# A recorded decoder trunk: projections that may pass each other in the plan, an inverse by 8-blocks, and work moved from VectorE to ScalarE and GpSimd

## The chip, the cores and the metric

The kernel runs on one core of a Trainium2 chip. The metric is the device time of one execution in microseconds (us): three executions of the kernel before took 4351.48, 4353.93 and 4364.67 us, the median is 4353.93 us. The change is one set of edits to one file; the shapes, the inputs and the outputs stay the same.

## The reference

One layer of a decoder trunk with two branches that read the same normalised input: a gated delta net with 8 heads of 128 (below: G) and an RWKV-7 branch with 16 heads of 64 (below: R), for a prompt of 16 + 2048 tokens and for 8 sample sequences of 4 tokens. The parts that matter here:

```python
h = rmsnorm(x, ln1_w)
p = jnp.einsum('btd,de->bte', h, w_in)           # one projection, 10384 columns wide
# branch A: causal convolution of 4 taps and SiLU on q, k, v; q and k normalised; decay g, beta
lower = where(strict, einsum('bnhik,bnhjk->bnhij', k_beta, k) * decay, 0.0)
t_inv = triangular_solve(eye + lower, eye)       # the inverse of a 64x64 unit triangle per chunk and head
# per chunk of 64 tokens, one after the other, with a state per head:
v_new = u_c - w_c @ s;  o = q_c @ s + qk_c @ v_new;  s = s * exp(gl_c) + kt_c^T @ v_new
# branch B, per token:  S = S diag(exp w) - (S kk)(kk*a)^T + v k^T,  y = S r;  group norm, bonus, gate
merged = gA * (o_a @ w_out_a) + gB * (o_b @ w_out_b)
y = rmsnorm(x + merged @ w_out, lnf_w)
```

The kernel computes the matrix products of the projections with three products of rounded halves: a number x is split into a high part (the same number, rounded to the matmul's format) and a low part (x minus the high part).

## The kernel before

**Work.** The 2064 prompt tokens are padded to 33 chunks of 64 and cut into five segments of 6, 6, 7, 7 and 7 chunks; the first carries the sample tokens too. In each segment the hidden rows are transposed and split into high and low tiles (`hHL`). Then come units: four G units (two heads each) and eight R units (two heads each). A unit has a projection stage (stage P: 128-column tiles of `w_in`, 24 matmuls each, into a PSUM tile `ps_p`), a stage M (normalisation, the chunk matrices, the inverse) and a chain C that goes through the segment's chunks one after the other (`ps_g` for G, `ps_c` for R). Gates, the two output projections and the final one follow as projection tiles.

**Weights** (`w_half`, L983). In the first segment a half tile of weights comes as raw numbers (`wr`); ScalarE rounds it to `wh`, and the low part `wl` is `wr` minus `wh`, a 128x512 subtraction: on VectorE for the first half of each tile, on GpSimd for the second. Both parts are then written to DRAM, and later segments load them from there.

**The split** (`split`, L962) of a 128-row tile `sq`, `kb`, `y` or `ysq`: a rounding copy into `sh` and a subtraction into `sl`, both on VectorE; two matmuls with a matrix of ones sum them over the partitions.

**The inverse** (`send_blocks`, L1357, and `g_inv`, L1369). The diagonal 16x16 blocks of all chunks and both heads of a unit are sent through DRAM so that each lies in one partition: 48 or 56 partitions of 256 numbers (`iM`). The tile `iD` is loaded with the identity from the constants. VectorE negates `iM`, and then finds row i of the inverse from the rows above it:

```python
for i in range(1, 16):
    self.tt(tmp[:NB, 0:i, 0:i], a, b, ALU.mult)
    nc.vector.tensor_reduce(Dk[:NB, 0, i, 0:i], tmp[:NB, 0:i, 0:i], AX.X, ALU.add)
```

GpSimd writes the transposed blocks beside, both go back through DRAM into `Dn` and `Dt`, and four rounds of small matmuls (`ps_n`, `Z`) make the 64x64 inverse out of them.

**The decay tile** of a G unit (in `g_g2`, L1433) is `EP`: a row of cumulated decays is loaded from DRAM into all partitions (`EP<-gcd`), VectorE subtracts a column `GT`, GpSimd adds a mask, ScalarE takes the exponential, VectorE multiplies by beta (a second `EP<-EP,GT`).

**What sets the order.** The operations are not issued as they are written. They are recorded as nodes, and a planner (`Sched`) walks through a model of time: each node has a cost by its engine, a node is ready when its inputs are there in the model, and each engine takes its best ready node (`pick`, L825; for TensorE `pick_pe`, L833). Pools of buffers are part of it. The order that comes out is then issued (`replay`, L894), and on the chip each engine goes through its own list strictly in that order. All instructions therefore carry the line of `replay` in the profile (L903), and are told apart by the names of their tiles.

TensorE knows kinds of matmuls: kind F (projections and other full-array rounded ones) and the small kinds. When `pick_pe` has finished a run of small ones, or has none worth a turn, it takes the next node of a projection tile. Committed projection tiles stand in the queue `s.pq`, some three or four of them. Only the tile at the head is looked at, and of it only the first node not yet started:

```python
if s.pq:
    for x in s.pq[0].pe:
        if not x.started:
            if x.nd == 0 and (not x.allocs or s.can(x)):
                pn = x
            break
```

A projection tile has four nodes of six matmuls, two for each half of its weights. A low-rank tile of an R unit (`lora`, `loral`) has one node of two matmuls and needs no weight buffer of the pool.

Of the kernel before, what the change touches and what calls it, by code (L numbers as in the profile page):

```python
# [4 lines left out]
F32 = mybir.dt.float32  # L5
# [3 lines left out]
ALU = mybir.AluOpType  # L9
AX = mybir.AxisListType  # L10
# [17 lines left out]
SEGMAX = 7  # L28
NT = 30
# [98 lines left out]
def plan(seq):  # L128
# [5 lines left out]
    for i in range(nseg):  # L134
        n = base + (1 if i >= nseg - extra else 0)
        t0, t1 = c0 * 64, (c0 + n) * 64
        p = max(0, pad - t0)
        segs.append(dict(i=i, nch=n, T=n * 64, pad=p, nreal=n * 64 - p, r0=max(t0 - pad, 0), last=False, smp=(i == 0)))
        c0 += n
# [307 lines left out]
class Sched:  # L447
# [385 lines left out]
    def pick_pe(s):  # L833
# [57 lines left out]
TWAIT = 3.0  # L891

# [13 lines left out]
class Trunk:  # L906
# [76 lines left out]
    def w_half(self, key):  # L983
# [8 lines left out]
        else:  # L992
# [3 lines left out]
            self.tt(wl, raw, wh.bitcast(F32), ALU.subtract, self.nc.gpsimd if key[1] else self.nc.vector)  # L996
# [27 lines left out]
    def setup(self):  # L1024
# [11 lines left out]
    def g_setup(self):  # L1036
# [48 lines left out]
        self.wbd = [P.tile([128, 2, 128], F32, name=f"wbd{i}") for i in range(1)]  # L1085
        self.xo = [P.tile([128, 2, 64], F32, name=f"xo{i}") for i in range(2)]
# [282 lines left out]
    def g_inv(self, sg, u):  # L1369
# [5 lines left out]
        M = self.p_i.tile([128, 16, 16], F32, tag="iM", name="iM", bufs=1)  # L1375
        nc.sync.dma_start(M[:NB], ex)
        Dk = self.p_i.tile([128, 2, 16, 16], F32, tag="iD", name="iD", bufs=1)
        io = CONST_LAYOUT["ID16"][0]
# [3 lines left out]
        tmp = self.p_i.tile([128, 16, 16], F32, tag="iT", name="iT", bufs=1)  # L1382
# [958 lines left out]
```

## Time and profile before

| | |
|---|---|
| time, median of 3 runs | 4353.93 us (4351.48 to 4364.67) |
| the profiled execution: its own time, its span | 4371.86 us, 4370.1 us |
| TensorE, matmuls | 4066.9 us busy, 93% of the span |
| VectorE | 2726.3 us, 62% |
| ScalarE | 1965.2 us, 45% |
| GpSimd | 992.3 us, 23% |
| mean granted TensorE clock | 0.941 of full speed |

The profiled execution is one execution with its own time, which is 17.9 us above the median; the trace numbers below are all its own. The page gives the time that an engine was busy. A matmul that runs while the granted clock is at half counts as busy for twice as long, so TensorE's 93% holds both useful time and time lost to the clock. The names: PE is TensorE, PEld its weight load, DVE is VectorE, ACT is ScalarE, POOL is GpSimd, SP the engine that issues the transfers. The five segments end at about 1000, 1780, 2560, 3440 and 4370 us.

### The profile page before, as it was taken

The numbers are of one execution on the slowest core, as the hardware profiler recorded it, in microseconds if no ns is written. First come the engines' busy times: TensorE is split into PE (matmuls) and PEld (weight loads), VectorE is DVE, ScalarE is ACT, GpSimd is POOL, SyncE is SP. The second block draws the span as 40 slices with busy tenths as digits, with TensorE's granted clock in tenths as the row PEclk, the third lists the DMA queues.
The fourth block names the chain that finished last, engine by engine and source line by source line (L and its number), as shares of the span: only waits on it lengthen the run. The fifth ranks groups of instructions, "written<-read, shape, count | busy, mean of one in ns | idle before, by whom it ended". The sixth has DMA issues, their size and how long they took to land. (4 is left out here: it accounts for less than half of the span.)

```text
span 4370.1 us, 91290 instructions
## 1 busy us (share of the span) xinstructions
PE 4066.9 (93%) x32684; PEld 3485.0 (80%) x32684; DVE 2726.3 (62%) x7052; ACT 1965.2 (45%) x4842; POOL 992.3 (23%) x1972
## 2 busy tenths in 40 slices
PE   6888999888999999999999999998998999999998
PEld 6767777778888888888788889787887887778887
DVE  6888677756576754557666645676763456666622
ACT  6544444525444443445444433554443334554431
POOL 3434233413121121212212121121121112111210
PEclk9889788979999999999999999999999999999999
DMA  7636465758745456864445567544445775444467
GB/s 254 201 117 203 136 199 172 243 171 279 235 145 154 137 166 211 263 201 148 126 127 157 172 223 261 159 139 131 128 151 170 237 239 151 128 140 137 143 221 256
DMA packets 660688, 790.09 MB, mean 181 GB/s; under 512 B 251105, under 2 KB 347209, under 8 KB 660234
## 3 DMA queue, kind: packets, MB, share of 16 engines
q1 hardware_dynamic: 660234, 784.25, 57.5%
q8 instruction: 259, 4.24, 0.4%
q14 instruction: 195, 1.60, 0.1%
HBM read 602.29 MB, written 180.56 MB: 179 GB/s over the span
## 5 line engine op out<-in xcount | busy, mean ns | idle before, releaser
L903 PE MATMUL ps_p<-hHL,wh 128*128 128x448 f32 (+3 forms) x7760 | 1828.1, 373 | 30.7 <-ACT wh L903 10.3
L903 PEld LDWEIGHTS ps_p<-hHL,wh 128*128 128x128 f32 x7760 | 1421.3, 195 | 156.1 <-issue 28.3
L903 PE MATMUL ps_p<-hHL,wl 128*128 128x448 f32 (+3 forms) x3880 | 911.6, 358 | 4.9 <-DVE wl L903 2.9
L903 PEld LDWEIGHTS ps_p<-hHL,wl 128*128 128x128 f32 x3880 | 730.2, 193 | 39.0 <-DVE wl L903 3.7
L903 POOL COPY xo<-X 64x64 f32<-64x64 f32 x528 | 172.4, 327 | 809.6 <-ACT X L903 380.1
L903 DVE TENSOR_TENSOR iT<-iM,iD 56x1 f32<-56x1 f32 (+1 forms) x900 | 295.5, 328 | 75.0 <-DMA iD<-in_consts 58.5
L903 ACT COPY raw<-ps_p 128x448 f32<-128x448 f32 (+3 forms) x285 | 144.2, 506 | 343.2 <-PE ps_p L903 313.8
L903 DVE SCALAR_TENSOR_TENSOR cv<-raw,pv,cv 128x448 f32<-128x448 f32 (+1 forms) x360 | 259.3, 720 | 56.0 <-ACT cv L903 48.6
L903 DVE TENSOR_REDUCE iD<-iT 56x1 f32<-56x1 f32 (+1 forms) x900 | 205.1, 228 | 17.7
L903 POOL TENSOR_TENSOR wl<-wr,wh 128x512 fp32r<-128x512 f32 x105 | 149.0, 1419 | 212.0 <-ACT wh L903 137.5
L903 ACT ACTIVATE X<-ps_c 64x64 f32<-64x64 f32 x264 | 55.5, 216 | 289.0 <-PE ps_c L903 124.2
L903 ACT CAST wh<-wr 128x512 fp32r<-128x512 f32 x210 | 128.3, 613 | 77.6 <-DMA wr<-in_wt 21.8
L903 ACT ACTIVATE X<-ps_c,dc 64x64 f32<-64x64 f32 x224 | 68.7, 307 | 207.2 <-DVE X L903 106.4
L903 DVE TENSOR_SCALAR X<-ps_c,dc 64x64 f32<-64x64 f32 x224 | 64.9, 291 | 135.0 <-PE ps_c L903 98.0
L903 ACT ACTIVATE sig<-cv 128x448 f32<-128x448 f32 (+2 forms) x120 | 67.3, 561 | 177.7 <-DVE cv L903 175.9
L903 PE MATMUL ps_p<-mhl,wh 128*128 128x448 f32 (+2 forms) x640 | 141.5, 359 | 5.7 <-ACT wh L903 4.5
L903 DVE TENSOR_SCALAR X<-ps_c 64x64 f32<-64x64 f32 x264 | 58.8, 227 | 131.1 <-PE ps_c L903 88.9
L903 DVE TENSOR_TENSOR Z<-Dt,ps_n 128x336 f32<-128x336 f32 (+1 forms) x180 | 66.9, 372 | 115.5 <-PE ps_n L903 100.0
L903 PE MATMUL ps_g<-gs,cv 128*64 128x128 f32 x1056 | 122.2, 308 | 17.0 <-DVE wbd L903 8.4
L903 PEld LDWEIGHTS ps_n<-Z,Wp 64*64 64x64 f32 x3168 | 109.9, 143 | 24.8 <-issue 9.5
L903 PE MATMUL ps_a<-RH,LH 64*128 64x128 f32 x1056 | 129.3, 292 | 0.0
L903 PE MATMUL ps_n<-Z,Wp 64*64 64x16 f32 (+1 forms) x3168 | 120.3, 220 | 7.7 <-DVE Z L903 5.8
(337 smaller groups left out, 7444.1 us busy)
## 6 DMA issues: line engine op xcount, KB each, us to landing
wh<-wh SPq DMA_DIRECT2D x1050, 256.0 KB
wl<-wl SPq DMA_DIRECT2D x1050, 256.0 KB
wr<-in_wt SPq DMA_DIRECT2D x210, 256.0 KB
gl<-gt SPq DMA_DIRECT2D x72, 224.0 KB
gt<-gt SPq DMA_DIRECT2D x48, 224.0 KB
xt<-in_x_prompt SPq DMA_DIRECT2D x29, 256.0 KB
xt<-in_x_prompt SPq DMA_DIRECT2D x13, 512.0 KB
out_y_p<-xt SPq DMA_DIRECT2D x26, 256.0 KB
```

Source lines behind the costliest of these rows:

```text
L903: getattr(getattr(nc, eng), name)(*[g(x) for x in a], **{q: g(x) for q, x in k.items()})
```

## The change

- **Planner.** `pick_pe` goes through up to `LOOK = 9` tiles of the queue, which is all of it, and takes the first whose next node is ready. A ready tile may pass one that is not, also between the halves of a tile.
- **Weights of the first segment.** All 210 low parts are now GpSimd's, where 105 were VectorE's.
- **Split.** The rounding copy `sh` goes from VectorE to ScalarE.
- **Inverse.** Seven steps make the inverses of both 8x8 halves of a 16x16 block at once; two products of 8x8 blocks (each in two pieces of 256 numbers, each a multiplication and a reduction) make the part below the diagonal. That is 11 multiplications and 11 reductions in place of 15 and 15. The identity is no longer loaded: GpSimd clears `iD` and writes the ones. The negation of `iM`, which waits for the transfer, is GpSimd's too.
- **Decay tile.** The subtraction, which waits for the transfer `EP<-gcd`, goes to GpSimd, and the mask's addition to VectorE.
- The numbers of two buffers (`NXO`, `NWB`) and the segment with the sample tokens (`SMP`) get names, with the values as before.

```diff
@@ pick_pe
-            if s.pq:
-                for x in s.pq[0].pe:
-                    if not x.started:
-                        if x.nd == 0 and (not x.allocs or s.can(x)):
-                            pn = x
-                        break
+            for p in s.pq[:LOOK]:
+                x = next(x for x in p.pe if not x.started)
+                if x.nd == 0 and (not x.allocs or s.can(x)):
+                    pn = x
+                    break
+LOOK = 9
@@ split
-        self.nc.vector.tensor_copy(h[:, :n], x)
+        self.nc.scalar.copy(h[:, :n], x)
@@ w_half
-            self.tt(wl, raw, wh.bitcast(F32), ALU.subtract, self.nc.gpsimd if key[1] else self.nc.vector)
+            self.tt(wl, raw, wh.bitcast(F32), ALU.subtract, self.nc.gpsimd)
@@ g_inv
-        nc.sync.dma_start(Dk[:NB, 0].rearrange("p a b -> p (a b)"), self.I["consts"][:NB, io:io + 256])
+        nc.gpsimd.memset(D0, 0.0)
+        nc.gpsimd.memset(D0[:, 0:256:17], 1.0)
         yield
-        nc.vector.tensor_scalar(M[:NB], M[:NB], -1.0, None, ALU.mult)
+        self.tt(M, M, self.eps[:NB, 4:5].unsqueeze(2).to_broadcast([NB, 16, 16]), ALU.mult, nc.gpsimd)
-        for i in range(1, 16):
-            a = M[:NB, 0:i, i].unsqueeze(1).to_broadcast([NB, i, i])
-            b = Dk[:NB, 0, 0:i, 0:i].rearrange("p m c -> p c m")
-            self.tt(tmp[:NB, 0:i, 0:i], a, b, ALU.mult)
-            nc.vector.tensor_reduce(Dk[:NB, 0, i, 0:i], tmp[:NB, 0:i, 0:i], AX.X, ALU.add)
+        for i in range(1, 8):
+            for_a = M2[:, :, 0:i, i].unsqueeze(2).to_broadcast([NB, 2, i, i])
+            for_b = D2[:, :, 0:i, 0:i].rearrange("p h m c -> p h c m")
+            tv = tmp[:NB, 0:2, 0:i, 0:i]
+            self.tt(tv, for_a, for_b, ALU.mult)
+            nc.vector.tensor_reduce(D2[:, :, i, 0:i], tv, AX.X, ALU.add)
             if i % 4 == 3:
                 yield
+        for q in range(2):
+            tv = tmp[:NB]
+            self.tt(tv, M[:, 0:8, 8 + 4 * q:12 + 4 * q]...to_broadcast([NB, 4, 8, 8]),
+                    D[:, 0:8, 0:8]...to_broadcast([NB, 4, 8, 8]), ALU.mult)
+            nc.vector.tensor_reduce(Xt[:NB, 4 * q:4 * q + 4], tv, AX.X, ALU.add)
+        yield
+        for q in range(2):
+            tv = tmp[:NB]
+            self.tt(tv, D[:, 8 + 4 * q:12 + 4 * q, 8:16]...to_broadcast([NB, 4, 8, 8]),
+                    Xt[:NB]...to_broadcast([NB, 4, 8, 8]), ALU.mult)
+            nc.vector.tensor_reduce(D[:, 8 + 4 * q:12 + 4 * q, 0:8], tv, AX.X, ALU.add)
@@ g_g2
-                self.tt(E3, E3, GT[:, :n, p].unsqueeze(2).to_broadcast([128, n, 64]), ALU.subtract)
-                self.tt(E3, E3, self.cst("MNEG").unsqueeze(1).to_broadcast([128, n, 64]), ALU.add, nc.gpsimd)
+                self.tt(E3, E3, GT[:, :n, p].unsqueeze(2).to_broadcast([128, n, 64]), ALU.subtract, nc.gpsimd)
+                self.tt(E3, E3, self.cst("MNEG").unsqueeze(1).to_broadcast([128, n, 64]), ALU.add)
```

Since costs and engines change, the planner's order changes nearly everywhere. Three places show what the text below speaks of.

**VectorE, first segment, in the middle of an inverse.** Before, the steps of one inverse (`iT` the products, `iD` the sums) stand between the work of other units, with a weight's low part among them:

```order
L903 TENSOR_TENSOR iT<-iM,iD 48x5x5
L903 SCALAR_TENSOR_TENSOR cv<-raw,pv,cv 128x384
L903 TENSOR_SCALAR X<-ps_c,dc 64x64
L903 TENSOR_REDUCE iD<-iT 48x5
L903 TENSOR_TENSOR wl<-wr,wh 128x512
L903 TENSOR_TENSOR iT<-iM,iD 48x6x6
L903 COPY rR<-ps_c 128x64
L903 TENSOR_REDUCE iD<-iT 48x6
```

In the change the seventh step is the last of its kind and the block products follow (`iX` is the intermediate 8x8 block):

```order
L905 TENSOR_TENSOR iT<-iM,iD 48x2x7x7
L905 TENSOR_TENSOR LH<-kb,cs 64x6x64
L905 TENSOR_REDUCE iD<-iT 48x2x7
L905 TENSOR_TENSOR RH<-sq,E 128x6x64
L905 TENSOR_TENSOR iT<-iM,iD 48x256
L905 COPY wbd_259<-ps_g 64x128
L905 COPY rR<-ps_c 128x64
L905 TENSOR_REDUCE iX<-iT 48x32
```

No `wl` stands on VectorE any more, and no `sh`; the chain's own instructions (`rR`, `X`, `wbd`) still stand between the steps of an inverse, behind fewer of them.

**GpSimd, first segment, where the first R chain runs.** `xo` are copies of an R chain's state that TensorE reads, `carA`, `rs`, `cvo` belong to the convolution. Before:

```order
L903 TENSOR_TENSOR wl<-wr,wh 128x512
L903 COPY cvo<-rs 128x24
L903 MEMSET mx_z 128x48
L903 COPY xo_260<-X 64x64 x6
L903 COPY iD<-iD 48x256
L903 COPY rs<-cvi 128x8x3
```

And in the change:

```order
L905 TENSOR_TENSOR wl<-wr,wh 128x512
L905 COPY xo_260<-X 64x64 x2
L905 TENSOR_TENSOR wl<-wr,wh 128x512 x2
L905 MEMSET mx_z 128x48
L905 TENSOR_TENSOR wl<-wr,wh 128x512
L905 COPY iD<-iD 48x256
L905 TENSOR_TENSOR wl<-wr,wh 128x512
L905 COPY xo_260<-X 64x64 x2
```

Six `xo` copies that stood side by side now have one to four low parts between them, and the copies of an R chain wait behind these.

**TensorE, first segment, a low-rank tile.** Before (numbers of the buffers are shown), the tile `ps_p_4340` is done before `ps_p_4491` starts, and the next tile starts after that:

```order
L903 MATMUL ps_p_4340<-hHL_936,wl_4314 128x376
...
L903 MATMUL ps_g_4334<-wbd0_259,ktl_3526 128x256
L903 MATMUL ps_p_4491<-lora0_1259,w2_4079 128x416
L903 MATMUL ps_p_4491<-loral_1277,w2_4079 128x416
L903 MATMUL ps_a_4503<-sh_4396,onesR_254 128x416
L903 MATMUL ps_a_4503<-sl_4423,onesR_254 128x416
L903 MATMUL ps_p_4513<-hHL_922,wh_4353 128x376 x2
```

In the change the tile `ps_p_4710` is half done when the low-rank tile `ps_p_4768` passes it:

```order
L905 MATMUL ps_p_4710<-hHL_926,wl_4603 128x368
...
L905 MATMUL ps_a_4757<-rAMs_3313,rVs_2265 64x32 x2
L905 MATMUL ps_g_4633<-wbd0_259,ktl_3176 128x256
L905 MATMUL ps_p_4768<-lora1_1269,w2_4007 128x416
L905 MATMUL ps_p_4768<-loral_1322,w2_4007 128x416
L905 MATMUL ps_p_4710<-hHL_934,wh_4654 128x368 x2
L905 MATMUL ps_p_4710<-hHL_935,wh_4654 128x368 x2
```

In TensorE's whole order of the change 57 of 611 projection tiles are broken off and taken up again after another tile, and none is before; in 52 of the 57 it is one low-rank tile of two matmuls that passes.

## Rows read from the trace of the kernel before

**Rows 1.** page, part 1: engine, busy us (share of the span) xinstructions

```profile
PE 4066.9 (93%) x32684; PEld 3485.0 (80%) x32684; DVE 2726.3 (62%) x7052; ACT 1965.2 (45%) x4842; POOL 992.3 (23%) x1972
```

**Rows 2.** windows, whole core: stretch, length, busy us (xcount) by engine, clock, DMA, GB/s

```profile
0.00:110.00 110.00, 73.35 (x407) 67.50 (x407) 66.55 (x163) 66.45 (x165) 38.09 (x100) 0.97 0.78 255
...
110.00:440.00 330.00, 279.34 (x2153) 235.82 (x2153) 273.95 (x740) 160.43 (x379) 128.81 (x242) 0.86 0.55 173
...
440.00:1000.00 560.00, 514.31 (x4403) 427.43 (x4402) 366.64 (x971) 240.05 (x610) 166.38 (x282) 0.85 0.58 185
...
1000.00:4370.10 3370.10, 3199.92 (x25726) 2754.28 (x25725) 2019.17 (x5181) 1498.31 (x3691) 659.01 (x1348) 0.96 0.58 178
...
1000.00:1780.00 780.00, 722.37 (x5933) 636.10 (x5933) 478.04 (x1272) 359.08 (x920) 173.07 (x350) 0.95 0.61 189
```

**Rows 3.** waits of PE: tile, releaser and tile, us in total, times, longest

```profile
PE ps_c L903 <- DVE X L903: 26.9, 22, 4.3
...
PE ps_p L903 <- ACT wh L903: 14.7, 7, 7.2
...
PE ps_g L903 <- DVE gs L903: 0.3, 1, 0.3
```

**Rows 4.** groups of DVE: xcount | busy us, mean ns | idle before, releasers

```profile
L903 DVE TENSOR_TENSOR iT<-iM,iD 56x1 f32<-56x1 f32 (+1 forms) x900 | 295.5, 328 | 75.0 <-DMA iD<-in_consts 58.5
...
L903 DVE TENSOR_REDUCE iD<-iT 56x1 f32<-56x1 f32 (+1 forms) x900 | 205.1, 228 | 17.7
...
L903 DVE TENSOR_TENSOR wl<-wr,wh 128x512 fp32r<-128x512 f32 x105 | 80.8, 770 | 27.3 <-DMA wl<-wl 10.7 <-ACT wh L903 9.4 <-DMA wh<-wh 3.0
...
L903 DVE CAST sh<-sq 128x448 fp32r<-128x448 f32 (+2 forms) x120 | 53.4, 446 | 16.0 <-ACT sq L903 13.8 <-PE ps_a L903 1.6
...
L903 DVE TENSOR_SCALAR iM<-iM 56x256 f32<-56x256 f32 (+1 forms) x60 | 17.0, 283 | 70.2 <-DMA iM<-ex 69.8
...
L903 DVE CAST sh<-y 128x448 fp32r<-128x448 f32 (+2 forms) x40 | 16.2, 405 | 4.4 <-ACT y L903 3.6
```

**Rows 5.** groups of DVE with shapes kept apart: steps of the inverse

```profile
L903 DVE TENSOR_TENSOR iT<-iM,iD 56x225 f32<-56x225 f32 x36 | 19.9, 553 | 0.7
...
L903 DVE TENSOR_TENSOR iT<-iM,iD 56x100 f32<-56x100 f32 x36 | 11.9, 330 | 0.7
...
L903 DVE TENSOR_REDUCE iD<-iT 56x15 f32<-56x225 f32 x36 | 13.6, 377 | 0.9
```

**Rows 6.** groups of DVE, 0 to 1000 us, then 1000 to 1780 us

```profile
L903 DVE TENSOR_TENSOR iT<-iM,iD 48x1 f32<-48x1 f32 (+4 forms) x180 | 71.6, 398 | 11.9 <-DMA iD<-in_consts 9.9
...
L903 DVE TENSOR_TENSOR iT<-iM,iD 48x1 f32<-48x1 f32 (+4 forms) x180 | 55.2, 307 | 17.0 <-DMA iD<-in_consts 13.4
```

**Rows 7.** groups of POOL, whole span

```profile
L903 POOL TENSOR_TENSOR wl<-wr,wh 128x512 fp32r<-128x512 f32 x105 | 149.0, 1419 | 212.0 <-ACT wh L903 137.5 <-PE ps_p L903 24.9 <-DMA wh<-wh 10.3
...
L903 POOL TENSOR_TENSOR Nt<-AL,consts 64x448 f32<-64x448 f32 (+1 forms) x80 | 92.6, 1157 | 150.1 <-DVE AL L903 94.7 <-PE ps_p L903 52.4 <-DMA ex<-AL 1.2
```

**Rows 8.** groups of ACT with shapes kept apart: a rounding copy

```profile
L903 ACT CAST hHL<-hHL 128x448 fp32r<-128x448 f32 x48 | 25.3, 564 | 31.1 <-DMA hHL<-oB 30.3 <-DMA hHL<-oA 0.5
```

**Rows 9.** waits of DVE, whole span

```profile
DVE iM L903 <- DMA iM<-ex: 69.8, 25, 9.3
...
DVE iT L903 <- DMA iD<-in_consts: 58.5, 13, 5.6
...
DVE EP L903 <- DMA EP<-gcd: 41.5, 11, 9.4
```

**Rows 10.** timeline: start us, us, engine, operation [idle before <-releaser]

```profile
2794.11 0.62 DVE L903 TENSOR_TENSOR EP<-EP,GT 128x448 f32<-128x448 f32 x1 [4.20 <-DMA EP<-gcd]
...
2796.99 0.69 PE L903 MATMUL ps_g<-gR,Z 64*64 64x128 f32 x4 [5.08 <-DVE gR L903]
```

**Rows 11.** groups of PE: the low-rank tiles

```profile
L903 PE MATMUL ps_p<-loral,w 64*128 64x448 f32 (+2 forms) x80 | 40.0, 500 | 0.0
```

More of the change, by code (lines that the diff above doesn't have):

```diff
@@ L28 @@
 SEGMAX = 7
+SMP = 0
+NXO, NWB = 2, 1
 NT = 30
@@ L137, in plan @@
         p = max(0, pad - t0)
-        segs.append(dict(i=i, nch=n, T=n * 64, pad=p, nreal=n * 64 - p, r0=max(t0 - pad, 0), last=False, smp=(i == 0)))
+        segs.append(dict(i=i, nch=n, T=n * 64, pad=p, nreal=n * 64 - p, r0=max(t0 - pad, 0), last=False, smp=(i == SMP)))
         c0 += n
@@ L1027, in setup @@
         nc.scalar.preload_act_table_set("natural_log_exp_and_others")
-        self.eps = P.tile([128, 4], F32, name="eps")
+        self.eps = P.tile([128, 8], F32, name="eps")
         nc.vector.memset(self.eps[:, 0:1], EPS)
@@ L1084, in g_setup @@
         nc.sync.dma_start(self.abd[1], abL.bitcast(F32))
-        self.wbd = [P.tile([128, 2, 128], F32, name=f"wbd{i}") for i in range(1)]
-        self.xo = [P.tile([128, 2, 64], F32, name=f"xo{i}") for i in range(2)]
+        self.wbd = [P.tile([128, 2, 128], F32, name=f"wbd{i}") for i in range(NWB)]
+        self.xo = [P.tile([128, 2, 64], F32, name=f"xo{i}") for i in range(NXO)]
         for w in self.wbd + self.xo:
@@ L1374, in g_inv @@
         NB = 8 * n
[L1375 to L1378, printed above, removed]
-        nc.sync.dma_start(Dk[:NB, 0].rearrange("p a b -> p (a b)"), self.I["consts"][:NB, io:io + 256])
-        yield
-        nc.vector.tensor_scalar(M[:NB], M[:NB], -1.0, None, ALU.mult)
-        tmp = self.p_i.tile([128, 16, 16], F32, tag="iT", name="iT", bufs=1)
@@ L1383, in g_inv @@
-        for i in range(1, 16):
-            a = M[:NB, 0:i, i].unsqueeze(1).to_broadcast([NB, i, i])
-            b = Dk[:NB, 0, 0:i, 0:i].rearrange("p m c -> p c m")
-            self.tt(tmp[:NB, 0:i, 0:i], a, b, ALU.mult)
-            nc.vector.tensor_reduce(Dk[:NB, 0, i, 0:i], tmp[:NB, 0:i, 0:i], AX.X, ALU.add)
+        PB = 272
+        Mt = self.p_i.tile([128, PB], F32, tag="iM", name="iM", bufs=1)
+        sq = lambda x: x[:, 0:256].rearrange("p (a b) -> p a b", b=16)
+        dg = lambda x: x.rearrange("p (h x) -> p h x", x=136)[:, :, 0:128].rearrange("p h (a b) -> p h a b", b=16)
@@ new lines, in g_inv @@
+        M = sq(Mt[:NB])
+        nc.sync.dma_start(M, ex)
+        Dt_ = self.p_i.tile([128, 2, PB], F32, tag="iD", name="iD", bufs=1)
+        D0 = Dt_[:NB, 0]
+        nc.gpsimd.memset(D0, 0.0)
+        nc.gpsimd.memset(D0[:, 0:256:17], 1.0)
+        yield
+        self.tt(M, M, self.eps[:NB, 4:5].unsqueeze(2).to_broadcast([NB, 16, 16]), ALU.mult, nc.gpsimd)
+        tmp = self.p_i.tile([128, 4, 8, 8], F32, tag="iT", name="iT", bufs=1)
+        Xt = self.p_i.tile([128, 8, 8], F32, tag="iX", name="iX", bufs=1)
@@ L1391, in g_inv @@
+        nc.gpsimd.tensor_copy(sq(Dt_[:NB, 1]), D.rearrange("p a b -> p b a"))
         yield
         bk = self.dr([8 * n, 2, 16, 16], "bk")
-        nc.sync.dma_start(bk, Dk[:NB])
+        nc.sync.dma_start(bk.rearrange("p w a b -> p w (a b)"), Dt_[:NB, :, 0:256])
         for w, dst in ((0, self.Dn), (1, self.Dt)):
@@ L1556, in g_g3 @@
             yield
-            w = self.wbd[0]
+            w = self.wbd[p % NWB]
             nc.scalar.copy(w[H[0], 0], pr[H[0]])
@@ L1937, in g_r3 @@
         y = self.t("y")
-        xo = self.xo[p % 2]
+        xo = self.xo[p % NXO]
         nc.scalar.copy(X[H[0], 0, 0], S[H[0]])
```

8 lines of the change are left out of this document (7 added, 1 removed).

## The prediction

> **What bounds the kernel now.** I read the page's first part, then the windows by stretch, then TensorE's waits, then the groups of the operations that the change touches. The first part shows TensorE busy for 4066.9 us of a span of 4370.1 [rows 1]. So 303 us are TensorE's idle time, and no edit of another engine can give back more than that, except through the clock. The windows add the clock [rows 2]: granted 0.97, 0.86, 0.85 and 0.96 in the four stretches. With the two levels 2.4 and 1.2 GHz, a mean of 0.85 means that 30% of the stretch ran at 1.2. Over the four stretches that makes 2 x (0.03x110 + 0.14x330 + 0.15x560 + 0.04x3370) = 537 us at the lower level. Work done there takes twice its time, so at most some 268 us more could be had.
>
> The windows also show where the engines differ. From 110 to 440 us VectorE is busy 274 of 330 us (83%) and TensorE is idle for 51: the first segment, with the weights to split and the sample sequences. From 440 to 1000 it is 65% and 46 us, after 1000 us 60% and 170 us of 3370. TensorE's waits name VectorE most: 38 rows of its list end in a VectorE instruction, from 26.9 us (`ps_c` behind `X`) to 0.3, and sum to 196 us. 17 rows end in ScalarE, the largest 14.7, and sum to 65 us [rows 3]. So TensorE is the bound, and what it loses, it loses mostly behind VectorE's queue.
>
> **The change part by part.**
>
> *Taken off VectorE.* Low parts: 105 x 0.770 = 80.8 us, all where weights are first used. Rounding copies: four groups, the first 120 x 0.446 = 53.4 us, the last 40 x 0.405 = 16.2, together 240 and 103.9 us. The inverse: 900 products of 295.5 us, 900 sums of 205.1 and 60 negations of 17.0, so 517.6 / 60 = 8.63 us each [rows 4]. For the new inverse I take the 56-partition shapes, between 330 ns for 100 elements and 553 for 225 [rows 5], which is 1.8 ns an element. Seven products of 2 to 98 elements come to 0.15 to 0.33 us, 1.6 together; four of 256 to 0.60 each, 2.4. The sums lie lower, 377 ns at 225 elements [rows 5]: seven of 0.14 to 0.24 make 1.3, four of 0.41 make 1.6. Together 6.9 us. The old one by the same shapes is 8.4 with its negation, so 1.5 us less, 92 us over 60. The decay tile exchanges a subtraction for an addition of the same size: nothing. In all VectorE loses 277 of 2726 us, 10%.
>
> *Put on others.* GpSimd: 105 x 1.419 = 149 us of low parts. A negation of 256 elements I take as two thirds of the 1.157 us of a 384- to 448-element product [rows 7], 0.7 us, and the two clearings at some 0.4: 60 x 1.1 = 66 us. ScalarE: 240 copies at 0.564 us by its rounding copy of the same size [rows 8], 135 us, 7% of its 1965.
>
> *What the waits do.* VectorE stood 69.8 us for the transfer `iM<-ex`, 58.5 more for `iD<-in_consts` and 41.5 for `EP<-gcd` [rows 9]. The identity's transfer is gone, and its wait with it. The other two I don't count as gone. GpSimd now waits for the transfer, but VectorE's next step of the same chain (the first product of the inverse, the addition of the mask) waits for GpSimd, and what is queued behind it on VectorE stays behind it. The trace shows the price: at 2789.9 us VectorE stood 4.20 us for `EP`, `gR` of another unit stood behind it, and TensorE idled 5.08 us for `gR` [rows 10]. Queued behind GpSimd's waits are the `xo` copies of the R chains and, in the first segment, low parts; TensorE waits for both.
>
> *What two engines do to each other.* The same 180 products of the inverse took 398 ns each in the first 1000 us and 307 in the next segment, though the shapes are the same [rows 6]. GpSimd was busy 33% of the first (38+129+166 us) and 22% of the second [rows 2]. I read 90 ns for 0.11 of GpSimd's time. The first segment gets about 0.14 more (89 of the 105 low parts by the windows' share, and 12 negations), so 115 ns on each product: 132 remain there, 15 us. They are about a third of the operations of that kind in the stretch, so I take 45 us given back, 15 from 110 to 440 and 30 from 440 to 1000. The ends are 15 and 63. The Trainium skill, page SBUF — State Buffer, section "SBUF: two separate sides", says that VectorE and GpSimd share a pair of ports by an exclusive lock: whichever of a GpSimd operation and a VectorE operation with two SBUF inputs starts first holds it for the whole instruction, and the other waits. The trace agrees in kind, by the 398 against 307 ns. By that rule alone the 140 us that GpSimd gains here would delay VectorE by its share of such operations, near a third, so 45 us; and the rule speaks against moving more.
>
> *The sum, by stretch.* Low parts spread as 9.6, 22.1, 35.4 and 13.8 us over the four stretches, copies as 1, 7, 12 and 83, inverses as 0, 9, 9 and 73.
> - 0 to 110 us: 11 us off VectorE; TensorE mostly waits for first transfers and rows. Ends 0 and 11, I take 4.
> - 110 to 440: 38 off, 15 back, 23 left. Ends 0 and 23; as VectorE is at 83%, three quarters, 17.
> - 440 to 1000: 56 off, 30 back, 26 left. Ends 0 and 26; at 65%, half, 13.
> - After 1000: 170 of 2019 off, 8.4%. About 118 of TensorE's idle 170 end in VectorE there (196 less the 78 of the same list cut at 1000 us). Ends 0 and 118; I take twice the relief in per cent, 17%, 20 us.
> - Clock: idle falls by 54 of 303 us, 18%. If the time at the lower level fell alike, 48 of 268. Ends 0 and 48; half, 24.
> - Passing: see the second rival; 2, ends 0 and 30.
> - ScalarE's 7% more on the 65 us behind it, doubled: 9 lost, ends 0 and 30. GpSimd's queue in front of `xo`: 5 lost, ends 0 and 68 (third rival).
>
> 4+17+13+20+24+2-9-5 = 66 us. The profiled execution's own time is 4371.86 us, so it would become 4306; it lies 17.9 us over the median of the runs, 4353.93, and from the median the forecast is 4288 us.
>
> **The rivals.**
>
> *The clock follows (4211).* If the first 1000 us came to the 0.95 of the next segment [rows 2], the time at the lower level there would fall from 2 x 0.14 x 1000 = 280 to 100 us, and half of the 180, 90 us, would be gained in place of some 13 counted above (24 x 280/537): 77 more. For it: VectorE's load falls just there. Against it: the sample sequences' small matmuls stay.
>
> *Passing is what counts (4240), or does nothing.* If a ready tile filled TensorE's waits in front of `ps_p`, which name weights and evacuation (14.7 us the largest [rows 3], 11 rows of some 55 together), up to 50 us would go. Against it: the order shows 57 broken tiles of 611, and in 52 of them only two matmuls of 0.5 us pass [rows 11]. 57 such passes fill at most some 57 us, and most stand where TensorE has other work. This part nearly doesn't do what it says.
>
> *Relief off the path (4350).* TensorE is the bound at 93%, VectorE's 38% of idle time shows that it is not; relief might be taken up by waits for TensorE itself (VectorE stands long behind `ps_c` and `ps_n`) and by the transfers that stay late. Then the gain is the clocked part of 110 to 440 alone, less ScalarE's loss: about nothing.
>
> *GpSimd becomes the first segment's bound (4400).* Six copies `xo` that stood together now have low parts between them. The first segment has 8 R units of 6 chunks, 48 steps; if each waits for one low part of 1.42 us, the chains are 68 us longer, and the collisions take 63 of the 95 us of relief there, so little is left against it; later segments gain 20. Net some 46 us slower. It decides if GpSimd, 129 of 330 us from 110 to 440, with 31 x 1.42 + 6 x 1.1 more 54%, passes the point where its queue is later than the chain; no row of TensorE's waits in front of `ps_c` names GpSimd now, so there is room.
>
> **How the numbers follow.** The forecast's case has 50%, with a range of its own of 4245 to 4330. The clock 15%, passing 5%, off the path 14%, GpSimd's queue 16%. 0.3% is about what a measurement of this kernel can tell from no change, 13 us. Faster by more: nearly all of the first three, 69, and 4 of the off-path case, 73%. The same: 10 from off the path and 1 of the rest, 11%. Slower: 16%. The range reaches up to the off-path case and down past the clock's: 4205 to 4364.
>
> **What would show it.** Right: VectorE near 2500 us busy, GpSimd near 1200, ScalarE near 2100; the first segment ending 35 to 60 us earlier; TensorE's idle after 1000 us down from 170 to about 150. The inverse's products and sums together near 6.9 us for each of 60. Waits for `iD<-in_consts` gone, waits of VectorE for GpSimd's `EP` and `iM` in place of the transfers'. Wrong: TensorE's waits naming GpSimd (`xo`, `wl`) by tens of us, or the first segment as long as before with GpSimd over 50%; a clock at 0.95 in the first 1000 us would mean that I have sized the gain too small.

## The result, and the profile after

The changed kernel took 4288.87, 4289.53 and 4292.19 us, and the kernel before beside it 4351.48 to 4366.08 (median 4359.3 of four). The ratio is 0.9842, 95% interval [0.9816, 0.9868]: 68 us or 1.6% faster, where 4288 us were forecast. (A fourth execution of the changed kernel took 10580.05 us, far outside all others, and is left out; the median with it is 4290.86.) The profiled execution took 4288.87 us, its span 4286.9.

The page's first part after, which answers to [rows 1]:

```profile
PE 4029.7 (94%) x32684; PEld 3457.3 (81%) x32684; DVE 2564.7 (60%) x6168; ACT 2081.1 (49%) x5082; POOL 1166.8 (27%) x2257
```

The span is 83.2 us shorter. 37.2 of it are TensorE's busy time, for the same 32684 matmuls, and 46.0 its idle time (303.2 before, 257.2 now). The medians are 68 us apart, not 83: the profiled execution of the kernel before took 12.6 us longer than the median beside the changed kernel. So up to some 15 us of what two traces differ by belongs to that execution and not to the change. The windows of the same stretches, beside [rows 2]:

```profile
0.00:110.00 110.00, 74.16 (x390) 64.58 (x390) 63.71 (x145) 65.64 (x164) 51.45 (x109) 0.97 0.76 242
110.00:440.00 330.00, 281.32 (x2193) 239.67 (x2194) 257.12 (x644) 166.32 (x396) 175.38 (x293) 0.84 0.55 172
440.00:1000.00 560.00, 515.98 (x4492) 436.49 (x4491) 364.25 (x864) 270.89 (x681) 244.68 (x368) 0.89 0.62 201
1000.00:4286.90 3286.90, 3158.30 (x25613) 2716.59 (x25611) 1879.64 (x4517) 1578.24 (x3844) 695.26 (x1489) 0.98 0.58 180
```

Up to 1000 us TensorE is idle for as long as before (128.5 us, 133.0 before), though VectorE and GpSimd changed most there; the clock is a little higher from 440 on. After 1000 us the idle time falls from 170 to 129 us, and the clock rises from 0.96 to 0.98. The ends of the first segment can be read from VectorE's scan that opens the second one, in the timelines (start us, us, engine, operation), first after, then before:

```profile
963.03 0.95 DVE L905 TENSOR_TENSOR_SCAN GB<-consts,g 8x384 f32<-8x384 f32 x1
```

```profile
989.09 0.94 DVE L903 TENSOR_TENSOR_SCAN GB<-consts,g 8x384 f32<-8x384 f32 x1
```

So 26 of the 83 us are gained by then, and 57 behind it. TensorE agrees: its 6963rd matmul ends at 1000.9 us before and at 974.8 after. TensorE's waits, beside [rows 3]:

```profile
PE ps_c L905 <- DVE rR L905: 19.2, 12, 5.7
PE ps_c L905 <- ACT X L905: 17.9, 21, 3.6
...
PE ps_p L905 <- POOL wl L905: 4.0, 3, 1.8
```

The rows that end in VectorE sum to 107 us (196 before), those of ScalarE to 81 (65), of DMAs to 53 (27), of GpSimd to 5 (1). VectorE gave back 89 us of TensorE's waiting, and others took 45. The groups that the change touches, of VectorE beside [rows 4], of GpSimd and ScalarE beside [rows 7, 8]:

```profile
L905 POOL TENSOR_TENSOR wl<-wr,wh 128x512 fp32r<-128x512 f32 x210 | 283.0, 1350 | 196.2 <-ACT wh L905 121.1 <-issue 26.2 <-PE ps_p L905 18.7
...
L905 DVE TENSOR_TENSOR iT<-iM,iD 56x2 f32<-56x2 f32 (+1 forms) x540 | 184.2, 341 | 82.2 <-POOL iM L905 71.0 <-POOL E L905 0.5 <-POOL iD L905 0.4
...
L905 DVE TENSOR_REDUCE iD<-iT 56x2 f32<-56x2 f32 (+1 forms) x540 | 126.4, 234 | 11.2
...
L905 DVE TENSOR_TENSOR iT<-iD,iX 56x256 f32<-56x256 f32 (+1 forms) x120 | 87.3, 727 | 2.2
...
L905 ACT CAST sh<-sq 128x448 fp32r<-128x448 f32 (+2 forms) x120 | 64.7, 544 | 3.2 <-DVE cs L905 1.3 <-DVE y L905 0.9
...
L905 DVE TENSOR_REDUCE iX<-iT 56x32 f32<-56x256 f32 (+1 forms) x120 | 48.9, 408 | 2.2
...
L905 POOL TENSOR_TENSOR iM<-iM,eps 56x256 f32<-56x256 f32 (+1 forms) x60 | 40.4, 674 | 113.2 <-DMA iM<-ex 109.9 <-ACT raw L905 3.1
```

One inverse takes (184.2 + 126.4 + 87.3 + 48.9) / 60 = 7.45 us on VectorE. Low parts (80.8), copies (103.9) and the inverse (517.6 - 446.8 = 70.8) make 255 us taken off VectorE; its busy time fell by only 162. About half of the difference is in the count: neighbouring instructions overlap at their ends, and busy time counts such a stretch once. The instructions' own times sum to 2988 us before and 2782 after, 206 less, so what is left there runs some 49 us longer. VectorE's waits, beside [rows 9]:

```profile
DVE sl L905 <- ACT sh L905: 97.7, 77, 8.3
DVE iT L905 <- POOL iM L905: 71.0, 27, 8.0
...
DVE EP L905 <- POOL EP L905: 31.3, 10, 6.6
```

All its waits for DMAs sum to 37 us (227 before), those for GpSimd to 130 (15 before). A new one, for ScalarE's copy `sh`, is the longest in total of those that don't end in TensorE.

### The profile page after: what moved, and what is told of

Read it like the earlier page. It is cut to its first block, busy times and chain, and to the rows that moved or that the text cites. A ratio compares the mean times of both kernels' runs of the same rounds, so it can differ in the third digit from the quotient of the medians.

```text
span 4286.9 us, 90688 instructions
## 1 busy us (share of the span) xinstructions
PE 4029.7 (94%) x32684; PEld 3457.3 (81%) x32684; DVE 2564.7 (60%) x6168; ACT 2081.1 (49%) x5082; POOL 1166.8 (27%) x2257
## 4 chain that ended last, share of the span: by engine, by line
PE 77%; DVE 8%; DMA 6%; issue 3%; ACT 3%; SPq 2%; POOL 1%; DVEq 0%; POOLq 0%; ACTq 0%
PE ps_p L905 51%; PE ps_a L905 10%; PE ps_c L905 6%; PE ps_g L905 5%; PE ps_n L905 4%; SPq L905 2%; DVE cv L905 2%; DMA wl<-wl 1%; DVE iT L905 1%; DMA EG<-gcd 1%; DVE X L905 1%; DMA Dt<-bk 0%; DMA bk<-iD 0%; DMA wh<-wh 0%; DVE LH L905 0%
## 5 line engine op out<-in xcount | busy, mean ns | idle before, releaser
L905 PE MATMUL ps_p<-hHL,wh 128*128 128x448 f32 (+3 forms) x7760 | 1853.0, 372 | 27.7 <-ACT raw L905 10.4
L905 PE MATMUL ps_p<-hHL,wl 128*128 128x448 f32 (+3 forms) x3880 | 920.9, 360 | 5.0 <-POOL wl L905 4.0
L905 POOL TENSOR_TENSOR wl<-wr,wh 128x512 fp32r<-128x512 f32 x210 | 283.0, 1350 | 196.2 <-ACT wh L905 121.1
L905 DVE TENSOR_TENSOR iT<-iM,iD 56x2 f32<-56x2 f32 (+1 forms) x540 | 184.2, 341 | 82.2 <-POOL iM L905 71.0
L905 ACT CAST wh<-wr 128x512 fp32r<-128x512 f32 x210 | 128.5, 613 | 77.1 <-POOL wl L905 19.6
L905 DVE TENSOR_REDUCE iD<-iT 56x2 f32<-56x2 f32 (+1 forms) x540 | 126.4, 234 | 11.2
L905 POOL TENSOR_TENSOR Nt<-AL,consts 64x448 f32<-64x448 f32 (+1 forms) x80 | 91.6, 1145 | 130.1 <-DVE AL L905 126.6
L905 PEld LDWEIGHTS ps_p<-mhl,wh 128*128 128x128 f32 x640 | 116.1, 191 | 13.2 <-ACT wh L905 4.9
L905 DVE SCALAR_TENSOR_TENSOR gs<-gs,gl,ps_g 128x128 f32<-128x128 f32 x264 | 83.6, 344 | 69.7 <-ACT vt L905 39.7
```

What stands on the lines that cost most here:

```text
L905: getattr(getattr(nc, eng), name)(*[g(x) for x in a], **{q: g(x) for q, x in k.items()})
```

## The experiments

At first two theories stood against each other. Queue theory: each step that leaves VectorE shortens TensorE's waits behind its queue. Order theory: the planner lays the whole program out anew for any change, and the new order moves the time by itself. The ratios are to the kernel before, run beside each kernel on the same chip (median 4356 to 4362 us).

**e1, e2: two orders of the same work.** e1 takes the look through the queue away, e2 changes one weight of the planner; both leave every instruction on its engine.

```diff
-LOOK = 9
+LOOK = 1
```

```diff
-BCH, BMX, BVL, AGE, ZUR = 2, 8, 1.5, 0.1, 0.5
+BCH, BMX, BVL, AGE, ZUR = 2, 8, 1.5, 0.11, 0.5
```

> The change with only the head of the queue looked at again (LOOK = 1); all else as in the change. Queue theory (the gain is VectorE's shorter queue): within 10 us of the change, 4281 to 4301 us, since only 57 of 611 tiles are passed. Passing theory: at least 30 us given back, 4320 to 4358. Order theory (any new order moves the time as much as the edits do): anywhere within 25 us of the change.

> The change with one weight of the planner for waiting time at 0.11 in place of 0.10; no operation, engine or cost differs, only the order. Queue theory: within 10 us of the change, 4281 to 4301 us. Order theory: 20 us or more away from it, to either side, as far as single edits move it.

e1: 4290.36 us, ratio 0.9838 [0.9813, 0.9862], as the changed kernel. The passing theory failed; the queue theory's band and the order theory's both held. e2: 4248.5 us, 0.975 [0.9725, 0.9775], 42 us faster than either: the queue theory's band failed here, the order theory's held. The first parts of their pages, e1 and then e2:

```profile
PE 4021.4 (94%) x32684; PEld 3436.7 (80%) x32684; DVE 2564.7 (60%) x6168; ACT 2068.4 (48%) x5082; POOL 1167.7 (27%) x2257
```

```profile
PE 3995.2 (94%) x32684; PEld 3430.7 (81%) x32684; DVE 2563.8 (60%) x6168; ACT 2071.9 (49%) x5082; POOL 1179.9 (28%) x2257
```

VectorE's load is the same to 1 us, and the instruction counts of all engines are equal. An order alone is worth 1%, part of it in TensorE's busy time (26 us), part in its idle time (the span of 4286.2 against 4243.3 leaves 17). Any single new layout has to be read with that in mind, e1 too: it shows no worth of passing, but some tens of us to either side could hide in its order.

**e3, e4: undo one part.** e3 puts the high copy back on VectorE; e4 puts the 15-step inverse back, with its operands cleared and negated on GpSimd as in the changed kernel.

```diff
-        self.nc.scalar.copy(h[:, :n], x)
+        self.nc.vector.tensor_copy(h[:, :n], x)
```

```diff
+        for i in range(1, 16):
+            fa = M[:, 0:i, i].unsqueeze(1).to_broadcast([NB, i, i])
+            fb = D[:, 0:i, 0:i].rearrange("p m c -> p c m")
+            self.tt(big[:NB, 0:i, 0:i], fa, fb, ALU.mult)
+            nc.vector.tensor_reduce(D[:, i, 0:i], big[:NB, 0:i, 0:i], AX.X, ALU.add)
```

> The change with the rounding copy of the split on VectorE again (240 copies, 104 us on VectorE, 131 us less on ScalarE). Queue theory: 15 to 40 us given back, 4305 to 4330, and more of TensorE's idle ends in VectorE. Rival (the copy only moved the wait: VectorE stands 98 us for ScalarE's copies in the change): no loss or a gain, 4270 to 4295. Order theory: within 25 us, either side.

> The change with the 15 steps of the 16-row inverse again; clearing and negation stay on GpSimd. Per inverse the change's VectorE work is 7.45 us where before had 8.35 without the negation, so VectorE is 55 to 90 us busier. Queue theory: 12 to 35 us given back, 4302 to 4325. Rival (the inverse's length is hidden, since other units run beside it): within 8 us of the change. Order theory: within 25 us, either side.

e3: 4243.39 us, 0.9733 [0.9707, 0.976], the fastest of all kernels here, with 97 us more on VectorE:

```profile
PE 4007.1 (95%) x32684; PEld 3435.5 (81%) x32684; DVE 2661.8 (63%) x6408; ACT 1963.9 (46%) x4842; POOL 1179.0 (28%) x2257
```

e4: 4306.15 us, 0.9869 [0.9845, 0.9894], 15 us slower than the changed kernel. e3 lies outside all three of its bands (the lowest began at 4266, 25 us below the changed kernel), e4 inside those of the queue and the order theory. Both differences, 47 and 15 us, are no larger, or hardly larger, than the 42 that e2 showed an order to be worth, so neither tells the part from its order.

**e5, e6: the move without the order.** These keep the plan of the kernel before row for row and change only the engine to which an instruction is issued: the planner still counts it as VectorE's. e5 moves the 240 high copies to ScalarE, e6 the 105 low parts to GpSimd.

```diff
+ISSUE = {"v_as_s": "scalar", "v_as_g": "gpsimd"}
-            getattr(getattr(nc, eng), name)(...)
+            getattr(getattr(nc, ISSUE.get(eng, eng)), name)(...)
```

```diff
-        self.nc.vector.tensor_copy(h[:, :n], x)
+        self.nc.v_as_s.copy(h[:, :n], x)
```

```diff
-            self.tt(wl, raw, wh.bitcast(F32), ALU.subtract, self.nc.gpsimd if key[1] else self.nc.vector)
+            self.tt(wl, raw, wh.bitcast(F32), ALU.subtract, self.nc.gpsimd if key[1] else self.nc.v_as_g)
```

> The kernel before with its own plan, row for row on every engine, but the 240 copies of the square's high part are issued to ScalarE where they stood on VectorE in the plan. No instruction changes its place on TensorE. Queue theory (VectorE's load is what TensorE waits for): about 104 us leave VectorE and about 130 us join ScalarE, which is idle for more than half the span; 10 to 30 us faster than before, 4332 to 4352. ScalarE theory (the copy on ScalarE ends later, because it queues behind evictions there, and VectorE's subtraction then waits for it): 10 to 50 us slower, 4372 to 4412. Order theory (the times of this work differ because the planner lays the whole program out anew, not because of the engine that does a step): nothing is laid out anew, so within 12 us of before.

> The kernel before with its own plan, row for row, but the 105 low parts of a weight that VectorE computed are issued to GpSimd. Queue theory: VectorE loses 81 us, GpSimd gains about 149; 8 to 25 us faster than before, 4337 to 4354. GpSimd theory (the low part comes later there and the projection waits for it, worst in the first segment): 5 to 40 us slower, 4367 to 4402. Order theory: within 12 us of before.

e5: 4347.12 us, 0.9975 [0.9963, 0.9987], by the ratio 11 us faster (5 to 16 by the interval). That is inside the band of the order theory and at the near end of the queue theory's. Its page's first part:

```profile
PE 4056.9 (93%) x32684; PEld 3476.6 (80%) x32684; DVE 2645.6 (61%) x6812; ACT 2074.3 (48%) x5082; POOL 974.3 (22%) x1972
```

VectorE's wait that is new there:

```profile
DVE sl L904 <- ACT sh L904: 78.4, 85, 6.2
```

VectorE's busy time falls by 81 us, and it now stands 78 us for the copy whose remainder it computes; TensorE's waits behind VectorE fall from 196 to 171. So the move is a small gain, not a loss: the ScalarE theory fell here.

e6: 4372.84 us, 1.0027 [1.0015, 1.0038], by the ratio 12 us slower. The queue theory failed; the time is at the edge of the order theory's band and inside the GpSimd theory's. The page's first part:

```profile
PE 4053.4 (93%) x32684; PEld 3472.7 (80%) x32684; DVE 2717.3 (62%) x6947; ACT 1967.0 (45%) x4842; POOL 1127.4 (26%) x2077
```

The 180 products of the inverse in the first 1000 us, which answer to the first of [rows 6]:

```profile
L904 DVE TENSOR_TENSOR iT<-iM,iD 48x1 f32<-48x1 f32 (+4 forms) x180 | 83.2, 462 | 12.2 <-DMA iD<-in_consts 10.1
```

80.8 us of low parts have left VectorE, and its busy time fell by 9.0. The same products in the same order went from 398 to 462 ns. The sums between them, which read one tensor and not two, did not change; here is their line in the same 1000 us, of the kernel before and then of e6:

```profile
L903 DVE TENSOR_REDUCE iD<-iT 48x1 f32<-48x1 f32 (+4 forms) x180 | 40.7, 226 | 2.0
```

```profile
L904 DVE TENSOR_REDUCE iD<-iT 48x1 f32<-48x1 f32 (+4 forms) x180 | 40.7, 226 | 2.2
```

Taken one by one in that order, VectorE's other 6947 instructions take 64 us longer in all, 59 of them in the first 1000 us; the rest of the 72 us is overlap, which busy time counts once. GpSimd's busy time of that stretch, from the windows:

```profile
0.00:1000.00 1000.00, 854.98 (x6947) 721.30 (x6948) 703.99 (x1780) 466.49 (x1149) 446.00 (x713) 0.87 0.59 188
```

It was 333 us before and is 446; VectorE's stays at 704 (707 before, the sum of the first three of [rows 2]) though 89 low parts, 67 us, are gone from it. What makes the 12 us is not settled by the traces: the profiled execution of e6 is even 3.5 us shorter than that of the kernel before, and TensorE's waits that end in GpSimd, the price that the GpSimd theory named, grew only from 1 to 6 us.

**e7, e8: is the spread the same elsewhere?** e7 is the kernel before in another order (the weight of age 0.15 in place of 0.1); e8 puts e3's edit and e2's together.

> The kernel before with one number of the planner changed (the weight of a unit's age in the choice of the next chain, 0.10 to 0.15): the same instructions on the same engines, laid out in another order. Order theory: the time moves by more than measurement, by up to 45 us to either side (4317 to 4407), most likely more than 13 us away from before. Queue theory: no engine's load is changed, within 13 us of 4362.

> The changed kernel with both edits that were faster alone: the square's high copy back on VectorE (4243 alone) and the weight of age 0.11 in place of 0.10 (4248 alone). If the copy's place is itself worth 47 us: 4248 less 47, 4195 to 4210. If both only drew another order from the same spread (order theory): no sum, between 4230 and 4295.

e7: 4385.94 us, 1.006 [1.0042, 1.0077], by the ratio 26 us slower than before with the same instructions. e8: 4283.57 us, 0.9823 [0.9809, 0.9837]: no sum, but 35 us slower than e2 and 40 slower than e3. The copy's place is not worth the 47 us that e3 seemed to show: with one weight of age undoing it gains 47, with the other it loses 35. The order theory held in both.

But it doesn't explain the result. The kernels in which no part of the change was planned anew stand at 1, 1.006, 0.9975 and 1.0027, and all those with its inverse at 0.9842 or less. A gap of over 1% is left, and the last four runs look for it.

**e9 to e12: the waits, or the load?** e9 is the kernel before with the decay tile's and the inverse's operand steps of the change alone (subtraction and negation on GpSimd, mask added on VectorE, identity cleared on GpSimd; the change's padded tiles `iM` and `iD` of 272 numbers come with it). The others undo parts of the changed kernel: e10 the subtraction, negation and mask, e11 the low parts, e12 the low parts and the high copies.

```diff
 e9, against the kernel before
-        nc.sync.dma_start(Dk[:NB, 0].rearrange("p a b -> p (a b)"), self.I["consts"][:NB, io:io + 256])
+        nc.gpsimd.memset(D0, 0.0)
+        nc.gpsimd.memset(D0[:, 0:256:17], 1.0)
-        nc.vector.tensor_scalar(M[:NB], M[:NB], -1.0, None, ALU.mult)
+        self.tt(M, M, self.eps[:NB, 4:5].unsqueeze(2).to_broadcast([NB, 16, 16]), ALU.mult, nc.gpsimd)
...
-                self.tt(E3, E3, GT[:, :n, p].unsqueeze(2).to_broadcast([128, n, 64]), ALU.subtract)
+                self.tt(E3, E3, GT[:, :n, p].unsqueeze(2).to_broadcast([128, n, 64]), ALU.subtract, nc.gpsimd)
...
```

```diff
 e10, against the changed kernel
-        self.tt(M, M, self.eps[:NB, 4:5].unsqueeze(2).to_broadcast([NB, 16, 16]), ALU.mult, nc.gpsimd)
+        nc.vector.tensor_scalar(M, M, -1.0, None, ALU.mult)
...
-                self.tt(E3, E3, GT[:, :n, p].unsqueeze(2).to_broadcast([128, n, 64]), ALU.subtract, nc.gpsimd)
+                self.tt(E3, E3, GT[:, :n, p].unsqueeze(2).to_broadcast([128, n, 64]), ALU.subtract)
...
```

```diff
 e11 and e12, against the changed kernel (e12 with e3's line as well)
-            self.tt(wl, raw, wh.bitcast(F32), ALU.subtract, self.nc.gpsimd)
+            self.tt(wl, raw, wh.bitcast(F32), ALU.subtract, self.nc.gpsimd if key[1] else self.nc.vector)
```

> The kernel before with one part of the change alone, planned anew: the decay mask's subtraction and the negation on GpSimd, the mask's addition on VectorE, the identity cleared on GpSimd in place of its DMA; the 15-step inverse, the shared low parts, the high copy on VectorE and the old rule for projection tiles stay. Waits theory (what the change gains is that VectorE no longer stands in its queue behind DMA landings, 227 us in all before, 37 after): most of the gain, 4280 to 4310. Load theory (the gain comes from the work taken off VectorE, which stays there here): 4335 to 4365. Either may be off by the 25 us or so that an order draws.

> The changed kernel with the subtraction and the negation back on VectorE and the mask's addition back on GpSimd (the identity is still cleared on GpSimd). Waits theory: VectorE waits for DMAs again, most of the gain is lost, 4320 to 4355. Load theory: 8-block inverse, low parts and copies are still off VectorE, 4260 to 4305.

> The changed kernel with every other low part of a weight back on VectorE. Load theory: 81 us return to VectorE, 10 to 30 us slower than the changed kernel, 4300 to 4320. Give-back theory (the frozen plan showed that VectorE's other work grows by about as much as the low parts took, as GpSimd works beside it): nothing is lost, 4250 to 4295, the spread of orders.

> The changed kernel without its two moves of load, the high copy and the low parts: what is left of the change is the 8-block inverse, the waits and the look through the queue. Load theory: 185 us more on VectorE, 30 to 60 us slower than the changed kernel, 4320 to 4350. Waits theory: nothing that counts is undone, 4230 to 4290, and with luck the fastest of all.

e9: 4318.87 us, 0.9903 [0.9883, 0.9923], 41 us faster than before. Its page's first part:

```profile
PE 4048.3 (94%) x32684; PEld 3455.2 (80%) x32684; DVE 2718.4 (63%) x6993; ACT 1964.9 (46%) x4842; POOL 1061.1 (25%) x2152
```

What is left of VectorE's waits for the two transfers that [rows 9] name besides the identity's:

```profile
DVE iT L905 <- POOL iM L905: 36.5, 19, 6.3
DVE EP L905 <- POOL EP L905: 24.6, 8, 6.6
```

VectorE is as busy as before (2718 against 2726 us). Its waits for DMAs fell from 227 to 59 us and those for GpSimd rose from 15 to 91, and TensorE's waits behind VectorE fell from 196 to 120, most of the way to the changed kernel's 107. So these waits fell without less work on VectorE. TensorE's whole idle time fell by less, 35 us (303 to 268), since its waits for ScalarE and for DMAs grew by 40. The time alone doesn't tell the theories apart (9 us past the waits theory's band, 16 short of the load theory's, either within an order's 25); the waits speak for the waits theory. The scan that opens the second segment starts as early here as in the changed kernel (963.03), without a low part moved; in e6, where they alone moved, it starts no earlier than before (989.09). First e9, then e6:

```profile
962.47 0.95 DVE L905 TENSOR_TENSOR_SCAN GB<-consts,g 8x384 f32<-8x384 f32 x1
```

```profile
991.26 0.94 DVE L904 TENSOR_TENSOR_SCAN GB<-consts,g 8x384 f32<-8x384 f32 x1
```

e10: 4264.51 us, 0.9785 [0.9766, 0.9805], 26 us faster than the changed kernel. Its page's first part:

```profile
PE 4011.1 (94%) x32684; PEld 3441.1 (81%) x32684; DVE 2574.9 (60%) x6228; ACT 2077.7 (49%) x5082; POOL 1141.7 (27%) x2197
```

The waits of VectorE for the two transfers are back:

```profile
DVE iM L905 <- DMA iM<-ex: 53.4, 24, 12.6
DVE EP L905 <- DMA EP<-gcd: 35.4, 12, 7.5
```

The waits theory as I had put it failed, and the load theory's band held: that the subtraction and the negation stand on VectorE again costs nothing that shows beyond an order's spread.

The traces show why VectorE's standing alone doesn't tell. Each of TensorE's waits for VectorE can be followed back along VectorE's own order, from the instruction that released it to VectorE's last standstill of over 150 ns, but no further than the instruction that ran when TensorE began to wait; of the two waits the shorter one counts. In the kernel before, 81 of the 196 us start so at the three transfers: 30 at `EP<-gcd`, 30 at `iM<-ex`, 21 at `iD<-in_consts`. In e10 VectorE stands 53 us for `iM<-ex` and 35 for `EP<-gcd`, but only 7 and 1 us of TensorE's waits start there; in the changed kernel 19 and 16 start at GpSimd's `iM` and `EP`. What such a standstill costs depends on what the layout has put behind it.

What e9 and e10 share against the kernel before is the identity without its transfer.

e11: 4273.2 us, 0.9807 [0.9785, 0.9829], 18 us faster than the changed kernel; the load theory failed and the give-back theory held. Its page's first part:

```profile
PE 4015.3 (94%) x32684; PEld 3446.8 (81%) x32684; DVE 2576.1 (60%) x6273; ACT 2078.1 (49%) x5082; POOL 1029.5 (24%) x2152
```

The inverse's products in the first 1000 us (groups of VectorE, busy us and mean ns), of e11 and then of the changed kernel:

```profile
L905 DVE TENSOR_TENSOR iT<-iM,iD 48x256 f32<-48x256 f32 (+7 forms) x108 | 41.0, 380 | 1.9 <-POOL iM L905 0.6
...
L905 DVE TENSOR_TENSOR iT<-iD,iX 48x256 f32<-48x256 f32 x24 | 17.0, 707 | 0.3
```

```profile
L905 DVE TENSOR_TENSOR iT<-iM,iD 48x256 f32<-48x256 f32 (+7 forms) x108 | 50.5, 468 | 6.2 <-POOL iM L905 4.2 <-POOL iD L905 0.4
...
L905 DVE TENSOR_TENSOR iT<-iD,iX 48x256 f32<-48x256 f32 x24 | 21.2, 884 | 0.2
```

With 105 low parts back on VectorE (76.8 us) its busy time is 2576.1 us, 11.4 more than without them. An order alone can move that by some 16 us (2726.3 before, 2742.6 in e7), yet not by 77: as in e6, most of what they took comes back in the operations beside them.

e12: 4272.07 us, 0.9794 [0.9771, 0.9817], 19 us faster than the changed kernel, against the load theory's 30 to 60 slower. Without either move of load the whole gain is there; the 19 us more lie within an order's spread.

## Why the prediction came out

The total was right (4288 forecast, 4289 to 4292 measured), the sign with it, and the forecast's own range of 4245 to 4330 held. The sum behind it was right in part only.

- **Loads.** GpSimd's 1167 and ScalarE's 2081 us came as forecast (near 1200 and 2100). VectorE was to lose 277 us of instructions; their own times fell by 206, its busy time by 162. The copies' term was near (103.9 us moved, 81 off the busy time in e5). The inverse was taken at 6.9 us and takes 7.45: its 256-element products with `iX` cost 727 ns and the others 656 on average, where I had drawn 600 from the 225-element shape. About 21 us of the 277 are that.
- **The step that failed: the low parts.** They stood in the sum as 80.8 us of relief, 67 of them in the first 1000 us, against 45 us that collisions with all of GpSimd's new work give back there, 63 at most. Measured alone, the low parts give back 64 us of busy time in that stretch (67 less the 3 from 707 to 704, e6), the end that I had set for everything, and 72 over the whole span (80.8 less 9.0); in the changed kernel it is 65 (76.8 less 11.4, e11, in another order). In e6 the time rose. So the first three stretches' 4 + 17 + 13 us had little of the low parts behind them. The second segment opens 26 us earlier, not 35 to 60, and it opens as early in e9, which shares the low parts as before, while e6, which moves them alone, gains nothing there (962.5 and 991.3 us). The observation under the term was right in kind: 90 ns on a product for 0.11 of GpSimd's time was read from two stretches, and in one stretch of one plan e6 shows 64 ns for 0.11. From the products' 15 us I went to 45, taking them for a third of the operations that lose. The losses are spread wider: the 180 products account for 11.6 of the 64 us by which e6's other instructions are longer.
- **The waits were named and had no term.** The prediction said that the identity's wait goes with its transfer, and that `EP` and `iM` would be waited for as before, now behind GpSimd. Both came so: `iD<-in_consts` is gone, 69.8 us for `iM` became 71.0, 41.5 for `EP` became 31.3 [rows 9], and putting these two back showed no cost in e10's layout. But the sum took TensorE's relief from VectorE's load alone, as twice the 8.4% (20 us after 1000 us). Measured there are 41 us less idle time, and e9 shows TensorE's waits behind VectorE falling by 76 us, its idle time by 35, with VectorE's load nearly unchanged. The identity's wait alone, which the prediction saw go, has 21 us of TensorE's waits behind it in the trace of the kernel before.
- **The clock** was taken at 24 us for a fall of the idle time by 54. The idle time fell by 46, and TensorE's busy time by 37 for the same matmuls, the granted mean going from 0.941 to 0.954. Half of the possible part was a fair choice, a little small, though an order alone moves TensorE's busy time by 26 us (e1, e2), so the 37 are not the clock's by themselves. The rival that the clock follows to 0.95 in the first 1000 us did not come: 0.84 and 0.89 there.
- **Passing** was priced at 2 us, and e1 shows 0 (4290.36 against 4290.86), as well as one order can show it.
- **ScalarE's 9 us lost** were not found: in the frozen order the copy's move gains 11 (e5), though the wait that I had not listed, VectorE's for `sh`, is 98 us in the changed kernel.
- **GpSimd as the first segment's bound** was the rival that e6 speaks for, in size far below its price: 12 us slower by the move of low parts, and TensorE waits 4.0 us for `wl` in the changed kernel, none for `xo`.
- **No term for the order.** The prediction treated the plan as if only the edits' own costs moved. The same instructions on the same engines took 4248 and 4291 us (e2, the changed kernel), 4357 and 4386 (before, e7), 4243 and 4284 (e3, e8). So a forecast for one new layout can't be better than some 20 us to either side. That it met the time within 3 us is luck in part: too much was credited to the low parts and nothing to the waits, two errors of opposite sign, and the draw of the order was not in the sum at all.

Where the 68 us are from, in steps that were each planned anew: the operand steps 0.9903 (e9), then the 8-block inverse and the look together 0.9794 (e12), then the two moves of load 0.9842. Eight kernels with the 8-block inverse lie at 0.9733 to 0.9842, the two with the old inverse and a cleared identity at 0.9869 and 0.9903, the two orders of the kernel before at 1 and 1.006. These three groups don't overlap, so I take the operand steps, with the identity's transfer in them, and the inverse's steps for the likely gain: 41 and 48 us by the steps above, of which the moves of load take back 21. That is argued and not shown. Two of the groups rest on two kernels, the nearest medians of the first two (the changed kernel and e4) are 15 us apart, less than an order's 42, and both kernels with the old inverse have the negation and the subtraction on GpSimd too. The identity was not run by itself; the 21 us that the trace of the kernel before shows behind it are half of the 41. e4 by itself gives the inverse 15 us. How they share the gain stays open, and so does what in an order makes the 42 us between e1 and e2.

The fastest kernel is e3, the change without the high copy's move: 4243.39 us, 0.9733. By e8 that is a good draw of an order more than a merit of the place.

## What to carry to other kernels

Where a planner lays out the whole program, price a move by a kernel that keeps the old layout and changes only the engine; otherwise the new order, here up to 1% of the time, is read as the move's worth. Waits in an engine's queue need a term of their own beside its load: count what the engine stands for in its own order, and follow the bounding engine's waits back to it, since the same standstill cost TensorE 30 us in one layout and 1 to 7 in another. Before moving elementwise work from VectorE to GpSimd, read how long the same VectorE operation takes in a stretch where GpSimd is busier: here the move bought next to nothing.

## What the hardware showed that I had not expected

Moving 105 subtractions of 128x512 from VectorE (770 ns each) to GpSimd (1394 to 1419 ns) left VectorE's busy time nearly where it was: 2726 to 2717 us in a fixed order. GpSimd's 135 us more made VectorE's other instructions 64 us longer, one for two. The products of two tensors lengthened, from 398 to 462 ns; the 900 sums of one tensor kept their 228 ns to the nanosecond. Not only operations with two tensors lengthened: the 24 `TENSOR_SCALAR` steps of `cv`, with one tensor and a column of scalars, went from 320 to 501 ns in the same run. Those of them that no GpSimd instruction overlapped took 231 ns in either trace, the others 410 ns on average before (12 steps) and 694 in e6 (14):

```profile
L903 DVE TENSOR_SCALAR cv<-rs,pv 128x32 f32<-128x32 f32 x24 | 7.7, 320 | 0.6 <-POOL rs L903 0.5
```

```profile
L904 DVE TENSOR_SCALAR cv<-rs,pv 128x32 f32<-128x32 f32 x24 | 12.0, 501 | 0.6 <-POOL rs L904 0.5
```

The Trainium skill, page SBUF — State Buffer, section "SBUF: two separate sides", says that of VectorE's operations those with two SBUF inputs, or in a mode that uses two ports, contend with GpSimd for the shared ports. The products' 398 to 462 ns and the sums' unchanged 228 agree in kind. Whether those 24 steps ran in such a mode the trace doesn't show. The share of a third that the prediction worked out under that rule was too small by these runs (64 of 135, near a half).
